# A decoder trunk's opening re-ordered: x loaded and transposed first, two conditioning blocks on TensorE, vector loads on GpSimd's queue, four gate tiles ahead

## Chip, cores and metric

One core of one Trainium2 chip. The metric is the device time of one execution in microseconds (us). A block is 128 of the 1024 model channels; there are eight.

## What is computed

One layer of a decoder trunk for 512 tokens of 1024 channels, all in float32. What matters here is its opening:

```
cond = silu(c);  sh1, sc1, gt1, sh2, sc2, gt2 = split(cond @ ada_w + ada_b)
h = rmsnorm(x, norm1_w) * (1 + sc1) + sh1
p = h @ w_in          # columns of mixers A (HGRN2), B (sparse attention), C (RWKV-7) and three gates
r, k, v, xw, xa, xg of mixer C = shift(p_c)     # p + (previous token's p - p) * mu
```

Then the three mixers run on `p`, their outputs are merged by sigmoid gates and projected, and a SwiGLU feed-forward part with a second conditioned norm follows.

## The kernel before

**Products.** A float32 product of full precision is made of three float32r products: a matrix is split into a high part (ScalarE's cast, `hi`) and the rest (VectorE's subtraction, `lo`), and hi x hi, hi x lo and lo x hi are added in PSUM (`mm3`). A weight tile of 128 output channels is therefore 8 x 3 = 24 products of 512 columns. Products of plain float32, as those with the vector `ones` or the small ones of the mixers, appear as two instructions each.

**The opening** (lines 575 to 607 of `run`, with `first_load`, `norm_x`, `first_gemm`, `modulate`). SyncE issues all loads: `c`, the conditioning weights of blocks 0 and 1 (`aw`, 1 MB a block: the columns of shift and scale, rows of 512 B), x in four row blocks, the identity, the vectors (`load_vecs`, twelve small loads in two groups), then for each further block `aw` and the 768 first columns of mixer C (`fw`, 0.4 MB), at the end constants and masks. Each row block of x is squared and summed on ScalarE, its `rs` taken to the power -0.5 on GpSimd, and scaled by VectorE and ScalarE in halves. For each of the 8 blocks VectorE forms the conditioning sums (`facc`, 8 steps of 256 columns), TensorE reduces them over the partitions by a product with `ones` (4 instructions a block), VectorE adds the bias and forms the scale `s`; TensorE transposes x's block, ScalarE applies scale and shift (`nh`) and casts (`hhi`), VectorE subtracts (`hlo`); then 18 products go into six PSUM tiles that stay open over all blocks. After the last block `c_setup` shifts the six results (ScalarE, then VectorE, for each) and applies tanh and sigmoid. In this part the framework's scheduler sets the order.

**The mixers** (line 1614 on, `manual_schedule`): the order is written out by the kernel's own planner. `Clock` keeps a planned time for each engine and buffer, from a table of costs (`count`, `spend`). `Order.run` advances *chains* (generators of narrow work: the mixers, the bias, the conditioning rows `D`, the compression `K`), each with a rank and a list of what it waits for, and *tiles* (`Weights`: load, split, 24 products) that fill TensorE in between. A chain goes first while the narrow work credited in `narrow` is below `pace`. `tend` loads up to three tiles ahead (three `wraw` buffers, two of `whi` and `wlo`) and splits the first one. A tile waits for the names in `needs`; a name is set by `mark`. The first tile is mixer A's `q` of head 0. Near the end of this part come eight tiles of the first gate (`gt`, they need `pm`, the room of the merged result) and eight compression tiles (`kt`, they need `blk`, and use their raw weights directly), in the order gt0, gt1, kt0, kt1, gt2, ..., gt5, gt6, gt7.

Of the kernel before, what the change touches and what calls it, by code (L numbers as in the profile page):

```python
# [100 lines left out]
FIRST = {k: 1 for k in range(KT)}  # L101


class Clock:
# [35 lines left out]
    def start(self, e, outs, ins):  # L140
        t = [self.ready(x) + 0.07 for x in ins] + [self.free(x) + 0.07 for x in outs]
        return max([self.at[e]] + t)

    def end(self, outs, ins, t, lag=0.0):
        for x in ins:
            for k in self.keys(x):
                self.read[k] = max(self.read.get(k, 0.0), t)
        for x in outs:
            for k in self.keys(x):
                self.wrote[k], self.by[k] = t + lag, lag > 0  # L150
        self.last = max(self.last, t + lag)

    def count(self, e, op, a, kw):
# [3 lines left out]
        t = self.start(e, outs, ins)  # L157
        n = max(int(np.prod(x.shape[1:])) for x in aps)
        if "dma" in op:
# [3 lines left out]
            self.bus = max(self.bus, t + 1.3) + size / 3.3e5  # L163
            return self.end(outs, ins, self.bus + 0.7)
# [43 lines left out]
class Order:  # L208
# [19 lines left out]
    def spend(self, o, l, r, turn=False):  # L228
# [11 lines left out]
        if kind != self.kind:  # L240
# [3 lines left out]

        t = max([clock.at["PE"]] + [clock.ready(x) + 0.07 for x in (l, r)] +
                [max(clock.read.get(x, 0.0), 0.0 if clock.by.get(x) else clock.wrote.get(x, 0.0)) + 0.07 for x in clock.keys(o)])
# [3 lines left out]
        clock.end([o], [l, r], t + c, 0.12)  # L250
# [11 lines left out]
    def mark(self, name, *aps):  # L262
        self.done[name] = max([self.at] + [self.clock.ready(x) for x in aps])
# [14 lines left out]
    def when(self, x):  # L278
        if isinstance(x, str):
            return self.clock.at["DVE"] - 0.1 if x == "dve" else self.room(x[1:]) if x[0] == ":" else self.done.get(x, 1e9)  # L280
        return self.clock.ready(x) if isinstance(x, bass.AP) else x
# [10 lines left out]
    def tend(self):  # L292

        loaded = sum(w.raw is not None and (w.w is None or w.split is None) for w in self.tiles)
        loaded += bool(self.steps and self.tile.split is None)
        for x, w in enumerate(self.tiles[:4]):
            if w.raw is None:
                if loaded >= 3:
                    break
                w.prepare(self.clock, 0)  # L300
                loaded += 1

        for x, w in enumerate(self.tiles[:3]):
            if all(n in self.done for n in w.needs):
# [3 lines left out]
        if self.tiles and all(n in self.done for n in self.tiles[0].needs):  # L308
            self.tiles[0].prepare(self.clock, 1)

    def job_ready(self):
        if self.steps:
            return 0.0
# [8 lines left out]
    def product(self):  # L322
# [4 lines left out]
        self.steps.pop(0)()  # L327
        self.narrow -= 0.8 * (self.at - t)

    def run(self, until=None, pace=4):  # L330
        while until not in self.done and (self.chains or self.tiles or self.steps):
# [23 lines left out]
class Weights:  # L355


    def __init__(self, load, split, steps, needs=(), ring="g"):
        self.load, self.split, self.todo, self.needs, self.ring = load, split, steps, needs, ring
        self.raw = self.w = self.hi = None  # L360

    def prepare(self, clock, split):
        if self.raw is None:
            self.raw = self.load()
        if split and self.w is None:
# [8 lines left out]
    def next(self, clock):  # L374

        return clock.ready(self.raw if self.hi is None else self.hi) - 0.2
# [8 lines left out]
class Trunk:  # L385
# [92 lines left out]
    def load_vecs(self, t, pool):  # L478
        nc, i = self.nc, self.i
        rows = self.t(pool, [sum(n for _, n in VTILES[t]), P], f"vrows{t}")  # L480
        for name, _ in VTILES[t]:
# [6 lines left out]
            nc.sync.dma_start(rows[r0:r0 + n], ap)  # L488
        return rows

    def turn_vecs(self, rows):
        nc = self.nc
        n = rows.shape[0]
        ps = self.psn()
        nc.tensor.transpose(ps[:, :n], rows, self.ident[:n, :n])
        vT = self.t(self.cp, [P, n], f"vT{len(self.vT)}")
        nc.vector.tensor_copy(vT, ps[:, :n])
        self.vT.append(vT)
        if len(self.vT) == 2:
# [4 lines left out]

    def setup_vecs(self):
        nc = self.nc

        self.cond = self.t(self.cp, [P, 8], "cond")
        nc.scalar.activation(self.cond, self.cT, AF.Sigmoid)
        nc.vector.tensor_tensor(self.cond, self.cond, self.cT, op=ALU.mult)  # L510
        self.adaT = self.t(self.cp, [P, 48], "adaT")
        self.mhalf = self.t(self.cp, [P, 8], "mhalf")
        nc.gpsimd.memset(self.mhalf, -0.5)
        self.ones = self.t(self.cp, [P, 1], "ones")
        nc.gpsimd.memset(self.ones, 1.0)
# [63 lines left out]
    def first_gemm(self, xs, pool):  # L579

        nc, V = self.nc, self.nc.vector
        h = self.h
        s1 = self.t(self.cp, [P, 8], "s1")
        offs = (1536, 1664, 512, 640, 0, 1024)
        pss = [self.psm(), self.psm(), self.psg(), self.psf(), self.psg(), self.psf()]
        pa, px = self.psn(), self.psn()

        def ada(k):
            if k not in self.first_a:
                return  # L590
            aw, n = self.first_a[k]
            acc = self.t(pool, [P, 2, 2, P], "facc", bufs=2)[:, :, :n]
            for kk in range(KT):
                self.ada_sum(acc, kk, aw[:, :, kk])
            for x in range(n):
                self.ada_cols(pa[:, 2 * (k + x):2 * (k + x) + 2], [acc[:, 0, x], acc[:, 1, x]], k + x, 8)
            V.scalar_tensor_tensor(s1[:, k:k + n], self.adaT[:, 8 + k:8 + k + n], 1.0, self.vec("norm1_w", k, n), op0=ALU.add, op1=ALU.mult)

        def products(ks):
            w = []  # L600
            for k in ks:
                raw = self.first_w[k]
                whi = self.t(self.wp, [P, 1024], "whi", F32R, bufs=2)
                wlo = self.t(self.wp, [P, 1024], "wlo", F32R, bufs=2)
                nc.scalar.copy(whi[:, :768], raw[:, :768])
# [1222 lines left out]
```

## Time and profile before

| | |
|---|---|
| median of 3 runs | 1171.03 us (1169.71 to 1173.94) |
| profiled execution | 1174.54 us, span 1172.6 us |
| mean granted TensorE clock | 0.983 of full speed |
| TensorE, VectorE, ScalarE, GpSimd busy | 96%, 56%, 35%, 7% of the span |

The span runs from the first to the last instruction of the profiled execution; its own time is 1.9 us longer. Times in rows are from the span's start. PE is TensorE, DVE is VectorE, ACT is ScalarE, POOL is GpSimd, SPq is the issue queue of SyncE. All engine calls but TensorE's go through a helper, so their line is L191 and products are L438; tiles are told apart by name. In a row `out<-in` names the tiles, `xN` the number of instructions merged into it, and what stands in brackets is the idle time ahead and what ended it. A product's shown duration is longer than the distance to the next one, because products are pipelined; the distance between starts is the pace.

### The profile page before, as it was taken

To read this page: it belongs to the slowest core of one execution; us is meant where nothing else is said; L and a number is where in the kernel's file an instruction comes from. 1 tells how busy PE (TensorE), PEld (TensorE's weight loads), DVE (VectorE), ACT (ScalarE), POOL (GpSimd) and SP (SyncE) were. 2 spreads that over 40 slices of the span, in tenths; PEclk is the share of its full clock that TensorE was granted. 3 is DMA by queue.
4 is the path that set the end of the run, shared out by engine and by line. 5 is a ranking of instruction groups with operands and counts; after the bars stand their busy time and mean duration, and the time that the engine had idled before them with its cause. 6 is when DMAs were issued, how large, how long until landed. Compare 5 with 4: busy or idle time off the path is not lost.

```text
span 1172.6 us, 18592 instructions
## 1 busy us (share of the span) xinstructions
PE 1120.2 (96%) x7497; PEld 912.0 (78%) x7497; DVE 656.4 (56%) x1396; ACT 412.0 (35%) x737; POOL 82.7 (7%) x96
## 2 busy tenths in 40 slices
PE   3989999999999999899999989998999999999997
PEld 3759887878887887577878758887888888888886
DVE  5858666666757766377666745446343343432533
ACT  4352421242332231155454654435232322322221
POOL 1001010120111000110112002110000000000000
PEclk9989999999999999889999999999999999999999
DMA  9934532324243244643222105542233333333231
GB/s 284 257 105 143 131 97 73 84 67 141 57 111 82 71 118 117 194 147 99 73 63 76 33 1 148 155 137 78 85 90 100 98 90 108 90 94 104 90 108 72
DMA packets 183086, 125.28 MB, mean 107 GB/s; under 512 B 27929, under 2 KB 163111, under 8 KB 183000
## 3 DMA queue, kind: packets, MB, share of 16 engines
q1 hardware_dynamic: 182424, 123.04, 37.0%
q8 instruction: 59, 0.97, 0.3%
q10 hardware_dynamic: 576, 1.05, 0.2%
q14 instruction: 27, 0.22, 0.1%
HBM read 121.15 MB, written 5.53 MB: 108 GB/s over the span
## 4 chain that ended last, share of the span: by engine, by line
PE 86%; DVE 4%; DMA 4%; SPq 2%; ACT 2%; issue 2%; POOL 0%; POOLq 0%; DVEq 0%; ACTq 0%
PE g L438 27%; PE f L438 27%; PE m L438 18%; PE n L438 11%; SPq L191 2%; PE n L442 2%; DMA adaw<-in_ada_w_dram 1%; DMA fw<-in_w_in_dram 1%; DMA wraw<-in_w_in_dram 1%; DVE wlo L191 1%; DMA x<-in_x_dram 1%; PE m L442 1%; ACT bpt L191 0%; DVE adacc L191 0%; DVE ylo L191 0%
## 5 line engine op out<-in xcount | busy, mean ns | idle before, releaser
L191 DVE TENSOR_TENSOR wlo<-wraw,whi 128x1024 fp32r<-128x1024 f32 (+2 forms) x144 | 164.1, 1139 | 158.3 <-ACT whi L191 156.5
L191 ACT CAST whi<-wraw 128x1024 fp32r<-128x1024 f32 (+2 forms) x144 | 139.1, 967 | 282.8 <-PE f L438 119.6
L438 PE MATMUL g<-hhi,whi 128*128 128x512 f32 x360 | 155.5, 432 | 9.6 <-ACT whi L191 9.6
L438 PE MATMUL g<-hhi,wlo 128*128 128x512 f32 x360 | 143.6, 399 | 1.9 <-DVE wlo L191 1.8
L438 PE MATMUL g<-hlo,whi 128*128 128x512 f32 x360 | 143.3, 398 | 0.0
L438 PEld LDWEIGHTS g<-hhi,whi 128*128 128x128 f32 x360 | 69.8, 194 | 29.5 <-ACT whi L191 10.9
L438 PE MATMUL f<-hhi,whi 128*128 128x512 f32 x232 | 91.8, 396 | 0.0
L438 PE MATMUL f<-hhi,wlo 128*128 128x512 f32 x232 | 90.9, 392 | 0.0
L438 PE MATMUL f<-hlo,whi 128*128 128x512 f32 x232 | 90.6, 390 | 0.0
L438 PEld LDWEIGHTS g<-hhi,wlo 128*128 128x128 f32 x360 | 69.0, 192 | 20.1 <-DVE wlo L191 4.7
L438 PEld LDWEIGHTS g<-hlo,whi 128*128 128x128 f32 x360 | 69.4, 193 | 11.4 <-issue 0.5
L191 DVE SCALAR_TENSOR_TENSOR adacc<-adaw,cond,adacc 128x512 f32<-128x512 f32 x56 | 42.5, 759 | 15.6 <-DMA adaw<-in_ada_w_dram 15.0
L438 PEld LDWEIGHTS f<-hhi,whi 128*128 128x128 f32 x232 | 44.3, 191 | 8.9
L438 PEld LDWEIGHTS f<-hhi,wlo 128*128 128x128 f32 x232 | 43.6, 188 | 9.0
L438 PEld LDWEIGHTS f<-hlo,whi 128*128 128x128 f32 x232 | 43.6, 188 | 8.5
L438 PE MATMUL f<-whi,hhi 128*128 128x256 f32 (+1 forms) x144 | 44.4, 308 | 0.0
L191 DVE CUSTOM_DVE_ANT_0 bs<-m,bW 128x128 f32<-128x128 f32 (+3 forms) x64 | 30.1, 486 | 24.5 <-PE m L438 15.3
L438 PE MATMUL f<-whi,hlo 128*128 128x256 f32 (+1 forms) x144 | 41.6, 289 | 0.0
L438 PE MATMUL f<-wlo,hhi 128*128 128x256 f32 (+1 forms) x144 | 41.5, 288 | 0.0
L438 PE MATMUL f<-yhi,whi 128*128 128x512 f32 x96 | 38.8, 404 | 2.2 <-ACT yhi L191 1.4
L191 ACT ACTIVATE bs<-bs,bst 128x128 f32<-128x128 f32 (+3 forms) x64 | 35.9, 563 | 12.9 <-DVE bst L191 12.4
L191 POOL TENSOR_TENSOR merged<-merged,msg 128x512 f32<-128x512 f32 x16 | 25.9, 1622 | 202.4 <-DVE msg L191 194.5
(439 smaller groups left out, 2376.8 us busy)
## 6 DMA issues: line engine op xcount, KB each, us to landing
wraw<-in_ffn_w_dram SPq DMA_DIRECT2D x66, 512.0 KB
wraw<-in_w_in_dram SPq DMA_DIRECT2D x52, 512.0 KB
adaw<-in_ada_w_dram SPq DMA_DIRECT2D x64, 256.0 KB
aw<-in_ada_w_dram SPq DMA_DIRECT2D x16, 512.0 KB
wraw<-in_w_branch_dram SPq DMA_DIRECT2D x16, 256.0 KB
wraw<-in_w_out_dram SPq DMA_DIRECT2D x8, 512.0 KB
fw<-in_w_in_dram SPq DMA_DIRECT2D x24, 128.0 KB
toep<-toep SPq DMA_DIRECT2D x8, 320.0 KB
```

Source lines behind the costliest of these rows:

```text
L191: r = f(*a, **kw)
L438: return self.nc.tensor.matmul(o, l, r, **kw)
L442: return self.nc.tensor.transpose(o, x, ident)
```

## The change

The planner now orders the opening too, as chains and tiles of the same kind. SyncE loads `c`, x and the identity first; the vectors are loaded from GpSimd's queue. Conditioning blocks 2 and 3, and 4 and 5, are formed in pairs (512 columns a step, loads of 1 KB rows); blocks 0 and 1 are not summed on VectorE but on TensorE, by 16 products of one column each. There are three buffers of two blocks' width, so the loads of block 4, 6 and 7 wait until blocks 0, 1 and 2 have been used. Row blocks 1 and 3 of x are squared on VectorE. All of x is transposed ahead into `xT`, and the modulation reads that. The products of a block stand as hi x hi, lo x hi and hi x lo in turn for all six results; in the last block they stand by result, and each result is shifted at its end (`c_first`). The first tile's split goes into buffers of its own (the later place of `bq`) as soon as the last scale exists; the bias chain waits for that tile. Four gate tiles lead, and the first may be split ahead of `pm`. `pace` is 8 instead of 4, and `mark` no longer counts TensorE's planned time. The planner's costs for transfers are changed as well.

```diff
-FIRST = {k: 1 for k in range(KT)}
+FIRST = {0: 1, 1: 1, 2: 2, 4: 2, 6: 1, 7: 1}
...
     def mark(self, name, *aps):
-        self.done[name] = max([self.at] + [self.clock.ready(x) for x in aps])
+        self.done[name] = max(self.clock.ready(x) for x in aps)
...
-    def run(self, until=None, pace=4):
+    def run(self, until=lambda: False, pace=8):
...
+            elif w.own and self.when(w.own) <= self.at:
+                w.prepare(self.clock, 1)
...
-            nc.sync.dma_start(rows[r0:r0 + n], ap)
+            nc.gpsimd.dma_start(rows[r0:r0 + n], ap)
...
-            for a in range(2):
-                nc.sync.dma_start(aw[:, a], ...)
+            for kk in ((0, 4), (4, 8)):
+                for a in range(2):
+                    nc.sync.dma_start(aw[:, a, kk[0]:kk[1]], ...)
...
+    def first_loads(self, pool, raw):
+        nc, last = self.nc, []
+        for k in range(KT):
+            if k in FIRST:
+                if len(last) > 2:
+                    yield f"a{last[-3]}"
+                last.append(k)
+                self.first_load(k, pool, True)
+            self.first_load(k, pool, False)
+        nc.sync.dma_start(self.consts, self.i["consts"][:, P:])
+        nc.sync.dma_start(raw, self.i["masks"])
+        yield raw
+        nc.gpsimd.tensor_copy(self.masks, raw)
+    def first_norm(self, xs, j, pool):
...
+        if j % 2:
+            V.tensor_tensor_reduce(self.t(pool, [P, D], "junk"), x, x, 1.0, 0.0, ALU.mult, ALU.add, ss)
+        else:
+            nc.scalar.activation(self.h[0][:, 2 * j:2 * j + 2].rearrange("p k t -> p (k t)"), x, AF.Square, accum_out=ss)
+        yield ss
+        self.rstd(rs, ss, 1.0 / D, 1e-6)
+        yield rs
...
+    def first_turn(self, xs):
...
+        yield self.ident, *(f"x{j}" for j in range(4))
...
+        for k in range(3):
+            turn(k, "mfg"[k])
+            keep(k)
+        for k in range(3, 6):
+            turn(k, "mfg"[k - 3])
+        yield "s0", ":n"
+        turn(6, "n")
+        turn(7, "n")
+        yield "hi0x"
+        for k in (5, 3, 4, 6, 7):
+            keep(k)
+        self.order.done["turned"] = self.order.at
+    def first_ada(self, pool, ks):
...
+            if k < 2:
+                ps = None
+                for q in range(2):
+                    for a in range(2):
+                        yield self.cond, aw[:, a, 4 * q:4 * q + 4], ("now", "turned")[k], ":n" if ps is None else "now"
+                        if ps is None:
+                            ps = self.psn()
+                        for kk in range(4 * q, 4 * q + 4):
+                            self.mm(ps[:, a:a + 1], aw[:, a, kk], self.cond[:, kk:kk + 1], start=(kk + a == 0), stop=(kk + a == KT))
+                self.order.done[f"a{k}"] = self.order.at
+                yield "vec0"
...
+    def first_tiles(self):
...
+                if k < KT - 1:
+                    return [(lambda q=q, x=x: (step(q, x), step(q + 1, x)), f"h{k}" if x == 2 else "now") for x in range(3) for q in (0, 2, 4)]
+                return [(lambda q=q: [step(q, x) for x in range(3)], f"h{k}") for q in range(6)]
...
+            order.chain("tx", self.first_turn(xs), 2)
+            order.chain("ada0", self.first_ada(p0, [0, 1]), 2.5, "m")
...
+            q = self.t(self.pbr, [P, 2, 1024], "bq", F32R)
+            order.job(self.a_tile("q", 0, h, (), (q[:, 0], q[:, 1])), af("f", 0), *av(0), ...
...
-            order.job(*gt[:2], *[x for n in range(4) for x in (kt[2 * n], kt[2 * n + 1], gt[2 + n])], *gt[6:])
+            order.job(*gt[:4], *[x for n in range(4) for x in (kt[2 * n], kt[2 * n + 1], gt[4 + n])])
```

## Rows read from the trace of the kernel before

**Rows 1.** The page, busy time of TensorE.

```profile
PE 1120.2 (96%) x7497; PEld 912.0 (78%) x7497; DVE 656.4 (56%) x1396; ACT 412.0 (35%) x737; POOL 82.7 (7%) x96
```

**Rows 2.** Windows: length, busy time by engine (x instructions), granted clock, DMA share, GB/s.

```profile
0.00:20.00 20.00, 2.95 (x13) 2.75 (x13) 9.81 (x29) 8.99 (x15) 2.97 (x11) 1.00 0.93 275
...
60.00:80.00 20.00, 14.62 (x54) 9.69 (x55) 10.10 (x16) 6.71 (x10) 0.12 (x1) 0.83 0.38 115
80.00:100.00 20.00, 19.37 (x136) 17.47 (x133) 15.27 (x22) 10.32 (x13) 5.73 (x7) 1.00 0.35 106
```

**Rows 3.** Timeline of TensorE in the opening: start, duration, what, idle before.

```profile
17.12 1.01 PE L438 MATMUL n<-ones,facc 128*128 128x1 f32 x4
...
21.61 1.12 PE L667 MATMUL n<-ident,x 128*128 128x128 f32 x4 [1.34 <-ACT nh L191]
...
22.38 1.20 PE L438 MATMUL m<-hhi,whi 128*128 128x512 f32 x2
...
42.76 0.50 PE L438 MATMUL n<-ones,facc 128*128 128x1 f32 x4
...
65.71 0.39 PE L438 MATMUL g<-hhi,wlo 128*128 128x512 f32 x1
...
66.16 0.39 PE L438 MATMUL f<-hhi,wlo 128*128 128x512 f32 x1
71.89 0.80 PE L438 MATMUL g<-hhi,whi 128*128 128x512 f32 x1 [5.34 <-ACT whi L191]
...
75.02 0.63 PE L438 MATMUL g<-hhi,whi 128*128 128x512 f32 x1
75.45 0.47 PE L438 MATMUL g<-hlo,whi 128*128 128x512 f32 x1
...
76.09 1.24 PE L438 MATMUL n<-bvg 33*8 33x512 f32 x4
```

**Rows 4.** Transfers to 70 us in slices of 1.75; timeline of SyncE, one issue.

```profile
GB/s 0 86 322 291 290 317 405 410 378 269 246 301 313 304 290 310 294 291 315 291 294 311 299 295 303 286 262 89 9 67 337 315 312 321 62 0 214 172 0 0
...
9.27 0.38 SPq L191 DMA_DIRECT2D vrows<-in_norm_w_dram  x1
```

**Rows 5.** Timeline and one window where gate and compression tiles meet.

```profile
475.21 1.04 ACT L191 CAST whi<-wraw 128x1024 fp32r<-128x1024 f32 x1 [5.95 <-DMA wraw<-in_w_in_dram]
476.31 0.80 PE L438 MATMUL g<-hhi,whi 128*128 128x512 f32 x1 [3.41 <-ACT whi L191]
...
476.31:482.15 5.84, 5.80 (x15) 4.22 (x16) 3.02 (x5) 0.00 (x0) 0.00 (x0) 0.53 1.04 307
...
496.64 0.37 ACT L191 ACTIVATE e<-f 62x256 f32<-62x256 f32 x1
...
506.17 0.86 PE L438 MATMUL n<-bw,e 128*128 128x64 f32 x6
```

**Rows 6.** Timeline and one window: 16 one-column instructions in a row, then the clock.

```profile
185.91 1.05 PE L438 MATMUL n<-ones,aq 128*128 128x1 f32 x8
...
186.82 1.03 PE L438 MATMUL m<-ones,adacc 128*128 128x1 f32 x8
...
188.00:190.00 2.00, 2.00 (x25) 1.39 (x25) 1.73 (x10) 0.58 (x1) 0.00 (x0) 0.57 0.08 31
```

**Rows 7.** Groups by line, to 66 us; GpSimd's `merged` and `adacc` from the page.

```profile
L191 DVE SCALAR_TENSOR_TENSOR facc<-aw,cond,facc 128x256 f32<-128x256 f32 x56 | 25.6, 482 | 0.6
...
L191 ACT ACTIVATE nh<-n,adaT,s 128x512 f32<-128x512 f32 x8 | 6.2, 777 | 19.8 <-DVE s L191 19.2 <-PE n L667 0.6
...
L191 ACT CAST hhi<-nh 128x512 fp32r<-128x512 f32 x8 | 5.0, 620 | 0.3
...
L191 POOL TENSOR_TENSOR rs<-rs,mhalf 128x1 f32<-128x1 f32 x4 | 2.6, 649 | 15.7 <-DVE rs L191 15.7
...
L191 DVE SCALAR_TENSOR_TENSOR adacc<-adaw,cond,adacc 128x512 f32<-128x512 f32 x56 | 42.5, 759 | 15.6 <-DMA adaw<-in_ada_w_dram 15.0
...
L191 POOL TENSOR_TENSOR merged<-merged,msg 128x512 f32<-128x512 f32 x16 | 25.9, 1622 | 202.4 <-DVE msg L191 194.5
```

More of the change, by code (lines that the diff above doesn't have):

```diff
@@ L292, in tend @@
     def tend(self):
-        loaded = sum(w.raw is not None and (w.w is None or w.split is None) for w in self.tiles)
+        loaded = sum(w.raw is not None and (w.w is None or w.split is None) for w in self.tiles if not w.early)
         loaded += bool(self.steps and self.tile.split is None)
@@ L307, in tend @@
                 break
-        if self.tiles and all(n in self.done for n in self.tiles[0].needs):
+        if self.tiles and (self.tiles[0].early or self.tiles[0].ahead or all(n in self.done for n in self.tiles[0].needs)):
             self.tiles[0].prepare(self.clock, 1)
@@ L312, in job_ready @@
         if self.steps:
-            return 0.0
+            x = self.steps[0]
+            return self.when(x[1]) if isinstance(x, tuple) else 0.0
         if not self.tiles:
@@ L326, in product @@
         t = self.at
-        self.steps.pop(0)()
+        x = self.steps.pop(0)
+        (x[0] if isinstance(x, tuple) else x)()
         self.narrow -= 0.8 * (self.at - t)
-    def run(self, until=None, pace=4):
-        while until not in self.done and (self.chains or self.tiles or self.steps):
+    def run(self, until=lambda: False, pace=8):
+        while not until() and (self.chains or self.tiles or self.steps):
             self.tend()
@@ L355, with __init__ @@
 class Weights:
-    def __init__(self, load, split, steps, needs=(), ring="g"):
-        self.load, self.split, self.todo, self.needs, self.ring = load, split, steps, needs, ring
+    def __init__(self, load, split, steps, needs=(), ring="g", early=False, own=None, ahead=False):
+        self.load, self.split, self.todo, self.needs, self.ring, self.early, self.own, self.ahead = load, split, steps, needs, ring, early, own, ahead
         self.raw = self.w = self.hi = None
@@ new lines, in first_mod @@
+    def first_mod(self, pool):
+        nc, h = self.nc, self.h
+        for k in range(KT):
+            yield f"s{k}", f"xT{k}"
+            f = self.t(pool, [P, T], "nh", bufs=2)
+            nc.scalar.activation(f, self.xT[k], AF.Identity, scale=self.s1[:, k:k + 1], bias=self.adaT[:, k:k + 1])
+            nc.scalar.copy(h[0][:, k], f)
+            self.order.mark(f"hi{k}", h[0][:, k])
+            self.order.done[f"hi{k}x"] = self.order.at
+            yield h[0][:, k]
+            nc.vector.tensor_tensor(h[1][:, k], f, h[0][:, k].bitcast(F32), op=ALU.subtract)
+            self.order.mark(f"h{k}", h[1][:, k])
@@ L712, in steps @@
             return [lambda k=k: step(k) for k in range(KT)]
-        return Weights(lambda: self.load_w(src, KT, P), lambda raw, hi: self.cut_w(raw, hi, KT, P), steps, needs)
+        return Weights(lambda: self.load_w(src, KT, P), lambda raw, hi: self.cut_w(raw, hi, KT, P, dst), steps, needs, ahead=early, own=f"s{KT - 1}" if dst else None)
     def proj(self, off, h, tag, n=128):
@@ L1131, in a_tile @@
         off = A_OFF + (0 if nm == "q" else 512) + 128 * hd
-        return self.full(self.i["w_in"][0, :, off:off + 128], h, end, needs)
+        return self.full(self.i["w_in"][0, :, off:off + 128], h, end, needs, dst)
     def a_mixer(self, y):
@@ L1608, in run @@
[L1608 to L1617 removed]
+            nc.scalar.activation(self.cond, self.cT, AF.Sigmoid)
@@ new lines, in run @@
+            kt, gt = self.b_compress_tiles(), self.gate_tiles(0, h)
+            order.job(*gt[:4], *[x for n in range(4) for x in (kt[2 * n], kt[2 * n + 1], gt[4 + n])])
+            order.run(lambda: f"h{KT - 1}" in order.done and not [w for w in order.tiles if w.early and w.w is None] and "vec1" in order.done)
+            ahead.close()
+            self.pc = pcs.enter_context(tc.tile_pool(name="pc", bufs=1))
+            with tc.using_default_side("right"):
+                self.pa = pas.enter_context(tc.tile_pool(name="pa", bufs=1))
```

322 lines of the change are left out of this document (173 added, 149 removed).

## The prediction, made before the change was timed

> **What bounds the kernel now.** I began with the page: TensorE is busy for 1120 of the 1172.6 us [rows 1]. So the change can give TensorE's idle gaps, and stretches in which products run at the lower clock. The windows show where these lie in the opening: 17 us of idle in the first 20, and 5.4 us between 60 and 80 at a mean granted clock of 0.83 [rows 2]. TensorE's timeline then says what they are. The first product of the opening starts at 22.38 and the last at 66.16; the next one, of the first mixer tile, has waited 5.34 us for ScalarE's `whi` and starts at 71.89 [rows 3]. Products follow each other every 0.225 us at 2.4 GHz (two steps from 65.71 to 66.16) and every 0.43 at 1.2 GHz (75.02 to 75.45) [rows 3]. The opening's 8 blocks of 18, 144 products, would take 32.4 us at the better pace and got 44.0; transposes, products of one column, waits and the clock are the rest. The transfers run at about 300 GB/s, and at 405 while x, with rows of 4 KB, is read [rows 4].
>
> After 80 us TensorE is nearly always busy (19.37 of 20 us [rows 2]), so a lead won in the opening should last unless a later gap swallows it. A later gap that the change touches stands where gate and compression tiles meet: 3.41 us of waiting before 476.31, then products at a granted clock of 0.53 [rows 5].
>
> **The start: x first.** Data begin to flow 3 us into the span [rows 4]. x is 2.1 MB, 5.2 us at 405 GB/s: it has landed near 9. Block 0 of the conditioning weights (1 MB, 3.5 us at 300 GB/s) follows, and its quarters land from about 10.2 to 12.9. From the planner's cost table in the code, used for the order alone, I read TensorE's order: three quarters of block 0's conditioning products, 24 transposes, the fourth quarter, 8 transposes, 12 products of block 0, all conditioning products of block 1, the other 6.
>
> A conditioning block is 16 products of one column, 32 instructions; four such took 1.01 us at the start and eight took 1.03 at the full clock, so 0.25 and 0.13 each [rows 3, 6]. Then: 24 at 0.25 from 10.2 end at 16.2; 24 transposes at 0.19 (four from 21.61 to 22.38 [rows 3]) at 20.8; the fourth quarter takes 1.0 to 2.0; two small VectorE steps about 0.5; `nh` and `hhi` 0.78 and 0.62 [rows 7]. The first product starts at 24.7 at the latest by this, at 23.0 if the clock rises during the transposes; I take 24.0, **1.6 us later than today**. TensorE's order sets it, not the transfers.
>
> **The blocks.** 144 products take 32.4 us. Six conditioning blocks stay on VectorE and leave 24 `ones` instructions, 0.125 each (four in 0.50 [rows 3]), 3.0 us; the second vector transpose 0.2. The transposes, today inside this stretch, are gone from it. New are block 1's 32 instructions, and here a row speaks against the change: after 16 of that kind in a row, from 185.91, the granted clock is 0.57 from 188 to 190 [rows 6]. So 20 of them count 0.13 and 12 count 0.25, 5.6 us (bounds 4.2 and 8.0), and 8 products behind them lose 0.2 each, 1.6 (0 to 3). The first 12 products follow a pause and can lose 2.4; I take 1.6. So the last product ends at 24.0 + 32.4 + 3.0 + 0.2 + 5.6 + 1.6 + 1.6 = 68.4 against 66.4 today: **+2.0 us**, between -3.6 (62.8) and +7.3 (73.7).
>
> What feeds this: VectorE's `facc` steps fall from 64 of 0.48 or less to 16 of 0.76 (as wide as `adacc`) and 16 narrow ones, 20 us instead of 30 [rows 7], and two squares of about 1.2 come in. The last conditioning data land near 47 us, the last scale follows near 50, and its products are due near 63: hidden. SyncE's queue now waits twice on TensorE, since block 4's weights take block 0's buffer and block 6's that of block 1: near 22 and 34 us, when the transfers ahead last until about 26 and 35. Behind the second wait stand blocks 6 and 7, constants, masks and the first tiles' weights, none due before 50. They cost nothing while they are that early; a wait longer by 10 us would be felt.
>
> **The vector loads on GpSimd.** Twelve small loads leave SyncE's queue (0.38 us to issue one [rows 4]) for GpSimd's, where no row shows a load. I bound one by 0.38 and by 1.62, GpSimd's costliest common instruction; I take 0.7, near the `rs` powers at 0.65, the smallest work there on loaded data [rows 7]. These four powers stand behind the loads, and all transposes wait for the last power. At 0.7 GpSimd is free at 9.3 and x normalised near 12.5; the transposes' turn is at 16.2, so nothing is lost up to 1.0 us a load.
>
> **The seam to the first tile.** Today six shifts, two functions and the tile's split follow one another on ScalarE and VectorE while TensorE waits. The change splits tile q0 into buffers of its own once the last scale exists, and shifts each product group as it ends. The gap, 66.4 to 71.89, is 5.5 us, and the low clock behind it cost 2.2: nine products from 71.89 to 76.09 took 4.2 where 2.0 would do [rows 3]. **-7.7 us**; at worst 2 us return as a wait for the second tile's split, which needs ScalarE and VectorE during the shifts. The bias products (1.24 us at 76.09 [rows 3]) move back and cost the same there.
>
> **The gates.** Four gate tiles instead of two lead, so the fourth one's weights need not wait for a buffer that compression tiles hold (its cast had waited 5.95 us for them [rows 5]). The gap of 3.41 can go, and of the 5.84 us of slow work after it (11 products, 4 transposes) about 2.7: -6.1. But one gate now follows the last compression tiles instead of three. That chain's tail lasts from the activation at 496.64 to its last products near 506.9 [rows 5]; one gate, 24 products or 5.4 us, leaves 4.9 open. I take **-1.2**, between -6.1 and +7.1 (gap kept, tail open, 2.2 of clock behind it). The other order rules (more narrow work before a tile's turn, marks without TensorE's time) add no instruction; they reshuffle the mixers, some us either way, priced at 0.
>
> **Sum.** +2.0 - 7.7 - 1.2 = -6.9 us against the profiled execution's 1174.5 (span 1172.6 and 1.9 around it), 1167.6; that execution stood 3.5 above the median of 1171.0, so **1164.1**.
>
> **The rivals.** *The clock, and slower.* The one-column products keep TensorE at 1.2 GHz, and block 1's bring it back there. If the first five blocks run so, 74 products beyond the 16 counted lose 0.2 each, and start and block 1 another 3.1: +17.9, 1182. From some 64 products at 1.2 GHz on, the whole is slower than before. For it: today's first products are slow, as are those after 71.89 and after the `ones` [rows 3, 6]. Against it: wide products brought the clock back within 3.6 us (71.89 to 75.45 [rows 3]). Chance 0.11.
>
> *GpSimd's queue.* At 1.62 a load it is free at 20.3, the powers end at 22.9, the transposes start at 23.6 instead of 16.2: +7.4, 1171.5. VectorE's work on x from 6 us on may lengthen the loads. The Trainium skill (SBUF — State Buffer, section "SBUF: two separate sides") says that loads issued by GpSimd can be held up while VectorE has the port that both share. No row here shows such a load. Chance 0.12.
>
> *The open tail,* the gap moved rather than closed: 8.3 more, 1172.4. For it: that chain is serial. Against it: other weights may be there to fill it. Chance 0.13.
>
> *The lead is given back in the mixers,* or q0's split comes late and the seam stays: 1171, from 1165 to 1177. For it, VectorE is busy for 15.27 of 20 us behind the seam; against it, TensorE is hardly idle there [rows 2]. Chance 0.16.
>
> **The numbers.** 0.48 is left for the forecast, 1158 to 1169 by itself. About 0.5%, 5.9 us, is what a measurement of this kernel can tell from no change: faster is below 1165.2, slower above 1176.9. The bounds of start, seam and gates, taken as independent about the sum, give 1156 to 1174; outside lie the clock rival and the far ends of the others. Faster, 0.50: most of the forecast, a third of the mixer case. Slower, 0.16: the clock rival and the far ends. The same, 0.34.
>
> **What would show it.** Right: one-column products ahead of the transposes, a first product near 24 and a last near 68, the next tile's product within 1 us of it, no gap at the fourth gate and a new one of some us behind the last compression tiles. Wrong: a first product after 28 (GpSimd, or the clock), products still 0.43 apart in the third block, or a lead of 5.7 us at 80 us that has shrunk at 470.

## The result, and the profile after

The changed kernel takes 1182.16 us (median of 5, 1179.88 to 1184.4) beside 1170.22 of the kernel before (median of 5): a ratio of 1.0087, with a 95% interval of 1.0065 to 1.0109 (the quotient of these two medians is 1.0102). The forecast was 1164.1, between 1156 and 1174; it had the sign wrong. The profiled execution took 1184.05 us, 9.5 more than the profiled one of before, at the same mean granted clock of 0.983.

The page has TensorE busy for 10.8 us more than before [rows 1]; over the span of 1182.3 us that leaves 51.3 us of idle time, where before had 52.4:

```profile
PE 1131.0 (96%) x7553; PEld 922.5 (78%) x7553; DVE 653.6 (55%) x1364; ACT 415.5 (35%) x740; POOL 89.4 (8%) x108
```

So, summed over the span, the time came as work on the engine that bounds the kernel. The idle time hardly shrank, because it moved. Where it went is seen when the span is cut at four points of both kernels, each the moment at which ScalarE begins to read a result: that of the first mixer tile (`q0`), of the last value tile, the first of the next stage, and the first of the feed-forward stage. Windows of the kernel before (length, busy time by engine, granted clock, DMA share, GB/s):

```profile
0.00:82.30 82.30, 56.60 (x247) 43.95 (x248) 53.27 (x122) 33.45 (x51) 4.06 (x13) 0.94 0.81 229
82.30:431.60 349.30, 345.01 (x3485) 292.12 (x3483) 233.98 (x522) 108.74 (x193) 38.62 (x43) 0.99 0.35 95
431.60:572.90 141.30, 134.70 (x1012) 101.42 (x1011) 91.25 (x242) 54.19 (x122) 10.37 (x15) 0.95 0.47 134
572.90:817.50 244.60, 236.00 (x1223) 186.82 (x1224) 141.81 (x349) 120.27 (x247) 27.45 (x21) 0.99 0.30 85
```

The same windows of the changed kernel:

```profile
0.00:84.10 84.10, 67.50 (x309) 55.38 (x310) 46.67 (x88) 41.02 (x59) 11.14 (x25) 0.94 0.69 216
84.10:442.90 358.80, 353.61 (x3706) 298.91 (x3706) 241.53 (x537) 106.70 (x192) 38.89 (x44) 0.99 0.36 96
442.90:589.60 146.70, 133.38 (x815) 99.27 (x816) 88.20 (x227) 54.06 (x122) 12.59 (x15) 0.95 0.44 129
589.60:826.90 237.30, 228.66 (x1195) 181.31 (x1196) 141.10 (x350) 118.30 (x245) 24.56 (x20) 0.99 0.30 86
```

The lengths of the middle windows can't be compared, since the order of products and mixers' steps differs (3706 instructions of TensorE stand in the second, 3485 before). The idle time, length less PE's busy time, can. Opening: 16.6 us instead of 25.7, with 10.9 more of busy time, so the first cut lies 1.8 later. Mixers: 5.2 instead of 4.3. From the last value tile to the next stage: **13.3 instead of 6.6**. Behind it 8.6 in both. Granted clocks are equal window by window. In the last three windows together TensorE is busy for 715.7 us in both, so 1.8 + 0.9 + 6.7 is 9.4, which is what the feed-forward stage starts late (826.9 against 817.5). A second profile of the changed kernel (part six) has 17.1, 4.1, 12.6 and 8.6 us of idle time: the longer end is there again, the 0.9 of the mixers is not.

The first cut needs care. TensorE itself is done with `q0` sooner than before, at 81.8 instead of 82.25 (first line: before), but ScalarE reads the result only 2.3 us later, when TensorE has long gone on:

```profile
81.86 0.39 PE L438 MATMUL g<-hhi,wlo 128*128 128x512 f32 x1
81.43 0.39 PE L448 MATMUL g<-hhi,bq 128*128 128x512 f32 x1
84.08 0.60 ACT L197 ACTIVATE aq<-g 128x512 f32<-128x512 f32 x1
```

The four bias products (1.2 us), which before stood inside `q0`, now come behind it. For the same work, then, the opening takes 0.7 us more: 9.1 less of idle time and 9.8 more of busy time.

**The opening.** TensorE's timeline (start, duration, what, idle before) answers [rows 3]:

```profile
10.57 5.25 PE L448 MATMUL n<-cond,aw 128*128 128x1 f32 x24 [0.15 <-DMA aw<-in_ada_w_dram]
...
20.40 0.95 PE L448 MATMUL n<-cond,aw 128*128 128x1 f32 x8
...
23.36 0.99 PE L448 MATMUL g<-hhi,whi 128*128 128x512 f32 x2 [1.07 <-ACT hhi L197]
...
25.62 3.63 PE L448 MATMUL n<-cond,aw 128*128 128x1 f32 x32
...
38.40 0.58 PE L448 MATMUL n<-ones,facc 128*128 128x1 f32 x4 [0.76 <-DVE facc L197]
39.23 0.61 PE L448 MATMUL n<-ones,facc 128*128 128x1 f32 x4 [0.25 <-DVE adaT L197]
41.78 1.22 PE L448 MATMUL g<-hhi,whi 128*128 128x512 f32 x2 [1.95 <-ACT hhi L197]
...
73.76 0.39 PE L448 MATMUL f<-hlo,whi 128*128 128x512 f32 x1
73.98 0.39 PE L448 MATMUL g<-hhi,bq 128*128 128x512 f32 x1
```

The first product starts at 23.36 and the next tile's follows the last one at once. Between them lies a hole: block 1's products end at 37.5, block 2's start at 41.78 and run at a granted clock of 0.50 until 47.06. The 64 conditioning instructions take 9.8 us. VectorE's and ScalarE's timelines say what block 2 waited for:

```profile
33.40 0.83 ACT L197 CAST whi<-fw 128x768 fp32r<-128x768 f32 x1 [2.25 <-DMA aw<-in_ada_w_dram]
```

```profile
26.51 0.96 DVE L197 TENSOR_TENSOR wlo<-fw,whi 128x768 fp32r<-128x768 f32 x1 [2.08 <-ACT whi L197]
...
34.26 0.96 DVE L197 TENSOR_TENSOR wlo<-fw,whi 128x768 fp32r<-128x768 f32 x1 [2.25 <-ACT whi L197]
35.14 3.11 DVE L197 SCALAR_TENSOR_TENSOR facc<-aw,cond,facc 128x512 f32<-128x512 f32 x4
...
40.06 0.16 DVE L197 SCALAR_TENSOR_TENSOR s<-adaT,vT 128x2 f32<-128x2 f32 x1
```

The last four sums of the pair 2 and 3 stand behind the cut of block 2's low half, and that cut waits for its high half, cast at 33.40. The row names a transfer, but there are two buffers for high halves, and block 0's products, which held the one that block 2 gets, end at 33.35. To 80 us VectorE stood still 13.6 us ahead of such cuts; in the same view of the kernel before (last line) this idle time is 0.0:

```profile
L197 DVE SCALAR_TENSOR_TENSOR facc<-aw,cond,facc 128x512 f32<-128x512 f32 x14 | 10.5, 749 | 0.3
L197 DVE TENSOR_TENSOR wlo<-fw,whi 128x768 fp32r<-128x768 f32 x8 | 7.7, 958 | 13.6 <-ACT whi L197 13.5
L191 DVE TENSOR_TENSOR wlo<-fw,whi 128x768 fp32r<-128x768 f32 x8 | 7.6, 953 | 0.0
```

**The end of the mixers.** What stood at [rows 5] stands 18 us later, and is longer. TensorE:

```profile
494.43 0.79 PE L448 MATMUL g<-hhi,whi 128*128 128x512 f32 x1 [4.69 <-ACT whi L197]
...
517.25 0.41 PE L452 MATMUL n<-ident,e 128*128 128x128 f32 x2 [1.88 <-DVE e L197]
...
532.69 0.48 PE L448 MATMUL m<-bkhi,bqs 128*128 128x128 f32 x1 [3.82 <-DVE bqs L197]
```

SyncE's queue and ScalarE at the first of these: the gate's load is issued at 487.01, behind loads of compression tiles, and cast at 493.34.

```profile
487.01 0.38 SPq L197 DMA_DIRECT2D wraw<-in_w_in_dram  x1
```

```profile
493.34 1.04 ACT L197 CAST whi<-wraw 128x1024 fp32r<-128x1024 f32 x1 [8.72 <-DMA wraw<-in_w_in_dram]
```

The second is the compression's tail: its transposes stand in TensorE's queue ahead of the last gate's remaining products, which wait with them. The third is for the next stage's queries, and no gate product is left to run in front of them.

### The profile page after: what moved, and what is told of

The parts are those of the page before. It is cut to its first block, busy times and chain, and to the rows that moved or that the text cites. A ratio compares the mean times of both kernels' runs of the same rounds, so it can differ in the third digit from the quotient of the medians.

```text
span 1182.3 us, 18697 instructions
## 1 busy us (share of the span) xinstructions
PE 1131.0 (96%) x7553; PEld 922.5 (78%) x7553; DVE 653.6 (55%) x1364; ACT 415.5 (35%) x740; POOL 89.4 (8%) x108
## 4 chain that ended last, share of the span: by engine, by line
PE 86%; DVE 4%; DMA 3%; ACT 2%; SPq 2%; issue 1%; POOL 1%; POOLq 0%; DVEq 0%; ACTq 0%
PE g L448 27%; PE f L448 27%; PE m L448 18%; PE n L448 11%; PE n L452 2%; SPq L197 2%; DMA aw<-in_ada_w_dram 1%; PE m L452 1%; DMA wraw<-in_w_in_dram 1%; DVE wlo L197 0%; DMA w2a<-in_nsa_pe_v_dram 0%; ACT bpt L197 0%; POOL aq L197 0%; DVE bs L197 0%; DMA bvg<-in_onehot_dram 0%
## 5 line engine op out<-in xcount | busy, mean ns | idle before, releaser
L197 DVE TENSOR_TENSOR wlo<-wraw,whi 128x1024 fp32r<-128x1024 f32 (+2 forms) x143 | 166.9, 1167 | 156.5 <-ACT whi L197 156.1
L448 PE MATMUL g<-hhi,whi 128*128 128x512 f32 x352 | 151.0, 432 | 9.6 <-ACT hhi L197 4.9
L448 PE MATMUL g<-hhi,wlo 128*128 128x512 f32 x352 | 138.5, 397 | 0.8 <-DVE wlo L197 0.7
L448 PE MATMUL g<-hlo,whi 128*128 128x512 f32 x352 | 138.4, 397 | 0.0
L448 PEld LDWEIGHTS g<-hhi,whi 128*128 128x128 f32 x352 | 67.4, 192 | 30.8 <-ACT hhi L197 6.0
L197 DVE SCALAR_TENSOR_TENSOR adacc<-adaw,cond,adacc 128x512 f32<-128x512 f32 x56 | 44.9, 802 | 22.9 <-DMA adaw<-in_ada_w_dram 22.5
L448 PEld LDWEIGHTS f<-hhi,wlo 128*128 128x128 f32 x232 | 43.8, 189 | 9.0 <-issue 0.2
L448 PE MATMUL f<-yhi,whi 128*128 128x512 f32 x96 | 39.1, 407 | 1.5 <-ACT yhi L197 1.4
```

The costliest lines, as they stand in the source:

```text
L197: r = f(*a, **kw)
L448: return self.nc.tensor.matmul(o, l, r, **kw)
```

## Experiments

Ratios are to the kernel before on the same chip, with their 95% intervals. They are not quotients of the medians and lie up to 0.24% beside them. Idle and busy times are TensorE's in the one profile of each run, between cuts at the same four results.

**One: the end of the mixers.** Four kernels, each with one edit. In the changed kernel, the gate order of before:

```diff
-order.job(*gt[:4], *[x for n in range(4) for x in (kt[2 * n], kt[2 * n + 1], gt[4 + n])])
+order.job(*gt[:2], *[x for n in range(4) for x in (kt[2 * n], kt[2 * n + 1], gt[2 + n])], *gt[6:])
```

> The changed kernel with the gate tiles in the order of before (two ahead, two at the end); all before the value tiles' end at about 420 us is unchanged. Theory (the loss is the tail: four gates ahead leave gate 5 unloaded and nothing beside the end of the compression and the next stage's preparation): the last sigmoid of the gates comes near 521 us instead of 531, the gap of 4.7 us in front of gate 5's products goes, and the time falls by 8 to 12 us, to 1170 to 1174. Rival pace (a pace of 8 lets the chains run ahead and the tiles lag, in whatever order the gates stand): 1180 to 1184, the last sigmoid still near 531. Rival opening (the loss is carried from the opening to the end): 1180 to 1184.

The kernel before with the reverse of that edit:

> The kernel before with four gate tiles ahead of the compression and none after it, nothing else. Theory: slower by 4 to 12 us (1175 to 1182), with a wait on a raw tile of weights in front of a late gate and the compression's tail uncovered. Rival pace: within 3 us of before, since at a pace of 4 the tiles are not late. Rival opening: within 3 us of before.

The pace, how much narrow work of the mixers may go ahead of a ready tile, at 4 again in the changed kernel (`pace=8` to `pace=4`), and at 8 in the kernel before:

> The changed kernel with the planner's pace at 4 again, in the opening and after it. Rival pace: 1170 to 1174, with the value tiles and the first gate 8 to 18 us earlier (first gate's sigmoid near 438 us, 455.6 now). Theory: the first gate comes earlier but gate 5 still waits for its load and the tail stays open: 1176 to 1183. Rival opening: 1180 to 1184.

> The kernel before with the planner's pace at 8 instead of 4. Rival pace: slower by 8 to 12 us, 1178 to 1182. Theory: within 4 us of before, since two gates still stand behind the compression and the next stage's preparation is covered. Rival opening: within 2 us of before.

Measured: 1184.59 us, 1.0099 (1.0071 to 1.0126), with the gate order back; 1186.07, 1.0118 (1.0086 to 1.0150), for the kernel before with four leading gates; 1183.75, 1.0092 (1.0065 to 1.0119), with the pace back; 1195.75, 1.0199 (1.0167 to 1.0230), for the kernel before at 8. Each part alone spoils the kernel before, by more than any answer had expected (at most 1182), and neither alone heals the changed one: my theory failed for the first run, the rival of the pace for the third. The rival of the opening came within a microsecond in these two and failed in the other two. The kernel before with four leading gates shows, wait for wait, the end that the changed kernel has:

```profile
492.36 0.79 PE L438 MATMUL g<-hhi,whi 128*128 128x512 f32 x1 [4.87 <-ACT whi L191]
...
516.27 0.41 PE L442 MATMUL n<-ident,e 128*128 128x128 f32 x2 [1.75 <-DVE e L191]
...
530.21 0.48 PE L438 MATMUL m<-bkhi,bqs 128*128 128x128 f32 x1 [3.80 <-DVE bqs L191]
```

Its idle time from the last value tile to the next stage is 13.4 us (6.6 before). At a pace of 8 the kernel before idles 9.0 us in the mixers and 12.2 behind them, and the mixers' clock falls to 0.95. To the feed-forward stage that is 9.7 us more of idle time and 11.6 more of busy time:

```profile
82.80:453.00 370.20, 361.20 (x3617) 306.53 (x3617) 241.34 (x536) 110.56 (x196) 39.31 (x43) 0.95 0.34 89
453.00:591.80 138.80, 126.55 (x871) 93.28 (x872) 83.20 (x227) 54.61 (x122) 10.05 (x15) 0.96 0.46 134
```

In the changed kernel with the gate order back the wait in front of a gate stays, and the idle time at the end is 13.2 us instead of 13.3:

```profile
488.64 0.80 PE L448 MATMUL g<-hhi,whi 128*128 128x512 f32 x1 [4.82 <-ACT whi L197]
```

With the pace back the gate's wait for its load is gone, but the waits of the tail and of the queries stay, at 1.95 and 3.82 us, and the idle time at the end is 12.2.

**Two: both edits undone together** in the changed kernel.

> The changed kernel with both the gate order of before and a pace of 4. Each alone gained nothing there, and each alone put into the kernel before cost 14 and 23 us. Theory now (either is enough to spoil the end of the stage, so only both together show it): 1165 to 1174, the last of the gates' sigmoids before 523 us and the next stage's first result near 573. Rival opening (the loss is carried from the opening, whatever stands at the end): 1179 to 1185 again.

Measured: 1180.81 us, 1.0041 (1.0017 to 1.0066). By the ratio half of the loss goes (by the medians two fifths: 1.0060 against 1.0102), less than expected. 13.2 us of idle time stay at the end, but of another kind: the gate's wait is gone, that for the queries is 1.21, and a chain's products wait for VectorE:

```profile
458.92 1.28 PE L448 MATMUL m<-X,GB 64*64 64x64 f32 x32 [3.66 <-DVE X L197]
```

The opening had to be looked at.

**Three: the opening,** on the kernel with both undone. First, the cut of a low half behind the sums of its own row:

```diff
-if self.tiles and (self.tiles[0].early or self.tiles[0].ahead or ...
+if self.tiles and (self.tiles[0].early in self.done or self.tiles[0].ahead or ...
...
-return [Weights(..., (f"hi{k}", "turned"), None, True) for k in range(KT)]
+return [Weights(..., (f"hi{k}", "turned"), None, f"a{k - (k in (3, 5))}" if k > 1 else "now") for k in range(KT)]
```

> As the run with both undone, but the low half of block 2's weights and of those behind it is cut on VectorE only after the sums that its own row waits for are done. Theory for the opening (VectorE's queue stood at a cut that waited for a buffer which the products of two blocks earlier held, with the pair's sums behind it): the first product of block 2, at 41.8 us in the changed kernel, comes 1.5 to 3 us earlier, the wait of 2.25 us for the high half goes from VectorE, and the last product of the opening, at 74.0, comes 1 to 4 us earlier. Rival (VectorE's sums themselves, or TensorE's lower clock, set the opening): block 2 within 1 us of 41.8, the last product within 1 us of 74.0.

Second, no pairs (`FIRST = {k: 1 for k in range(KT)}`, and six buffers of one block in place of three of two):

> As the run with both undone, but no pairs: every block's conditioning is loaded and summed by itself, blocks 0 and 1 still on TensorE. Theory for the opening (a pair's sums must all be done before the first of its two blocks can go on, and VectorE comes to them late): block 2's first product 3 to 5 us before 41.8 and the last product of the opening before 72. Rival (the pair saves VectorE 0.2 us in each of 14 steps and larger packets bring the loads earlier, so single blocks are dearer): the last product at 75 or later.

Third, block 1's conditioning back on VectorE:

```diff
-            if k < 2:
+            if k < 1:
...
-order.chain("ada0", self.first_ada(p0, [0, 1]), 2.5, "m")
-for k in list(FIRST)[2:]:
+order.chain("ada0", self.first_ada(p0, [0]), 2.5, "m")
+for k in list(FIRST)[1:]:
```

> As the run with both undone, but only block 0 has its conditioning on TensorE and block 1's sums go back to VectorE. Theory for the opening (VectorE is the engine that is late, so 3.7 us more on it delay everything behind): the last product 2 to 5 us later than in the run with both undone. Rival (the 32 narrow products between block 0's halves, 3.6 us on TensorE, and the lower clock behind them are what costs): the last product 1 us or more earlier, and a granted clock above 0.91 from 20 to 40 us.

Measured: 1179.11 us, 1.0041 (1.0017 to 1.0066); 1183.4, 1.0077 (1.0053 to 1.0100); 1182.64, 1.0061 (1.0033 to 1.0089). The totals differ too little to judge by; the openings don't. With the cut behind the sums VectorE (first fence) finishes the pair 2.7 us sooner, but the products of one column (TensorE, second fence) now stand behind block 1's:

```profile
32.42 3.10 DVE L197 SCALAR_TENSOR_TENSOR facc<-aw,cond,facc 128x512 f32<-128x512 f32 x4
35.44 0.95 DVE L197 TENSOR_TENSOR wlo<-fw,whi 128x768 fp32r<-128x768 f32 x1
```

```profile
37.49 0.62 PE L448 MATMUL f<-hlo,whi 128*128 128x512 f32 x2
37.95 0.50 PE L448 MATMUL n<-ones,facc 128*128 128x1 f32 x4
...
41.26 1.22 PE L448 MATMUL g<-hhi,whi 128*128 128x512 f32 x2 [1.95 <-ACT hhi L197]
```

Block 2 comes only 0.5 us sooner (the rival's answer), the last product 2.6 (the theory's, 71.4 against 74.0): the clock came back at 44 instead of 47, the later waits shrank. What is left of the hole is no longer VectorE's queue: 3.3 us lie between the first products of one column (37.95) and block 2's first product (41.26), a chain of two such sums, bias, scale, modulation and cast. Without pairs the last product ends at 75.9, so the pairs are not shown to be the fault. With block 1 back on VectorE it ends at 72.7, 1.5 before the 74.2 of the kernel it was put in, where I had expected 2 to 5 later: for block 1's work TensorE, to which the change moves it, was the dearer place. The clock was not the reason: from 20 to 40 us it was 0.87, and 0.91 in the changed kernel. Single profiles scatter: in the eight with the opening as changed the last product ends between 73.9 and 75.7. So 71.4 and 72.7 are clear of that, and 75.9 hardly is.

**Four: another pace.** The gate order of before with a pace of 5; with the two mends of the opening besides; four leading gates at a pace of 5; and the mended opening, gate order of before, at 7.

> The changed kernel with the gate order of before and a pace of 5, which lays the mixers' products out in an order nearer to that of before (about 80 per cent of TensorE's instructions stand in the same order, 70 with a pace of 4 or 8). Theory (the end of the mixers, where the chains and the tiles must run out together, decides, and the opening with its seam is worth about nothing): level with before, a ratio of 0.997 to 1.003, chain C's last result near 466 us and the last gate near 521. Rival (the loss is carried from the opening): a ratio of 1.004 to 1.010, as with the other paces.

> As the last, with the opening mended in two places: only block 0's conditioning on TensorE, and the low halves of blocks 2 and on cut behind the sums that they wait for. Theory: the opening's last product comes 2 to 4 us before that of the last run, q0's tile ends before 81 us, and the time is 2 to 4 us less, below before: ratio 0.993 to 1.000. Rival (what the opening gains, the mixers give back, as with the seam): the same time as the last run within 1.5 us.

> The changed kernel with a pace of 5 alone: four gate tiles lead, none stands behind the compression. Against the run with the gate order of before and the same pace it tells the price of the gate order alone. Theory: 4 to 12 us slower than that run (the kernel before lost 14 with this order), the next stage's first tile end (573 us before) 8 to 15 us later, with a wait of over 3 us on a gate's load. Rival (the pace is the whole cause): within 2 us of that run.

> The mended opening and the gate order of before, but a pace of 7 in place of 5. Theory (the pace decides how far the tiles run ahead of chain C, and any pace that ends the two apart loses): chain C's last result after 475 us, a stretch of TensorE under 16 of 20 us between 440 and 480, and 4 to 10 us slower than with a pace of 5. Rival (pace matters little once the opening is mended): within 2 us of that run.

Measured: 1186.56 us, 1.0085 (1.0050 to 1.0120); 1176.04, 1.0023 (1.0001 to 1.0046); 1182.54, 1.0074 (1.0051 to 1.0096); **1166.91, 0.9954 (0.9930 to 0.9978)**. An order like that of before did not bring the time of before, and at 5 the gate order of before gained nothing (1186.56 against 1182.54 with four leading gates; the rival had named a difference within 2 us). The mended opening was worth 0.6%, TensorE ending `q0` at 77.4 instead of 83.6. The last run I had expected to lose, and it is the fastest: chain C ends late, at 473 us, near the 475 that I had named, but the tiles are so early (last value tile at 411.8) that TensorE finds work: it is busy for 18.4 and 18.8 of the 20 us on either side of 460, not under 16. Its windows:

```profile
0.00:80.60 80.60, 64.26 (x281) 52.08 (x282) 50.70 (x96) 41.00 (x58) 11.19 (x25) 0.94 0.71 226
80.60:411.80 331.20, 328.47 (x3254) 279.54 (x3253) 224.11 (x508) 100.58 (x182) 38.67 (x41) 1.00 0.37 97
411.80:568.90 157.10, 147.78 (x1252) 112.12 (x1251) 102.66 (x258) 59.20 (x132) 14.62 (x17) 0.98 0.45 133
568.90:809.70 240.80, 231.79 (x1209) 184.15 (x1210) 141.42 (x348) 118.29 (x245) 26.97 (x21) 0.99 0.30 86
```

16.3, 2.7, 9.3 and 9.0 us of idle time, 37.4 to the feed-forward stage against 45.2 before and 43.8 in the changed kernel, and its busy time of 772.30 is that of before again. Against the mended opening at a pace of 5 the gain is not idle time, which was 38.1 us there, but busy time, which was 781.0, at granted clocks of 0.98 and 0.96 in the two middle windows where the fastest kernel has 1.00 and 0.98.

**Five: the shares.** From the fastest kernel one part is taken back each time: the opening (as changed, unmended); pace and gate order (the mended opening alone in the changed kernel); the gate order. The fourth is the kernel before at a pace of 7.

> The changed kernel with its own opening, the gate order of before and a pace of 7: the fastest run so far without the mended opening. Theory (the opening as changed costs 3 to 5 us against the mended one, and the rest is the order at the end): 3 to 6 us slower than the fastest run, a ratio of 0.998 to 1.002 to before. Rival (the end alone decides): 0.993 to 0.997, as that run.

> The changed kernel with the mended opening alone; pace 8 and four leading gate tiles stay. Theory: q0's tile ends 3 to 4 us before the changed kernel's 84.1, and the time is 3 to 6 us below it, a ratio of 1.003 to 1.006; TensorE's idle time from the last value tile to the next stage's first result stays near 13 us. Rival (the opening is the whole loss): 0.996 to 1.000. Rival (what the opening gains is given back): 1.007 to 1.010.

> The fastest run (mended opening, pace 7) with the four leading gate tiles of the change again. Theory (four in front leave nothing beside the end of the compression): 3 to 10 us slower than the fastest run, a wait of over 3 us on a late gate's high half and one of over 3 us on the queries of the next stage. Rival (with the tiles early enough the gate order is free): within 2 us of it, 0.993 to 0.997.

> The kernel before with a pace of 7 instead of 4, nothing else. Theory (its order was the fitting one at 4, as the 23 us lost at 8 showed): slower by 5 to 20 us, a ratio of 1.004 to 1.017. Rival (7 is the better pace whatever the opening): 0.990 to 0.997.

Measured: 1174.42 us, 1.0017 (0.9994 to 1.0041); 1177.65, 1.0048 (1.0027 to 1.0070); 1175.68, 1.0021 (0.9997 to 1.0045); 1189.0, 1.0146 (1.0111 to 1.0180). All four ratios lie where the theory said. The pace alone doesn't do it, and each part has its price: the opening 0.63% of the time (1.0017 less 0.9954), four leading gates 0.67%, and pace 8 instead of 7 another 0.27% (1.0048 less 1.0021; these intervals overlap). TensorE's time to the feed-forward stage, in us, from one profile each:

| kernel | idle | of it at the end of the mixers | busy |
|---|---|---|---|
| before | 45.2 | 6.6 | 772.3 |
| changed | 43.8 | 13.3 | 783.1 |
| fastest | 37.4 | 9.3 | 772.3 |
| fastest with the opening as changed | 37.9 | 9.1 | 774.8 |
| fastest with four leading gates | 42.2 | 14.1 | 775.5 |
| mended opening alone | 42.2 | 13.4 | 778.6 |
| before, pace 7 | 51.0 | 6.7 | 780.9 |

In these profiles the gates' price is idle time at the end (4.7 us more). The opening's is mostly work, but that profile, at 1169.8 us, lies 4.6 under the median of its kernel and shows only a part of it.

TensorE with four leading gates, and the fastest run, at the same places:

```profile
482.74 0.80 PE L448 MATMUL g<-hhi,whi 128*128 128x512 f32 x1 [3.27 <-ACT whi L197]
...
522.10 0.47 PE L448 MATMUL m<-bkhi,bqs 128*128 128x128 f32 x1 [3.80 <-DVE bqs L197]
```

```profile
488.49 0.50 PE L448 MATMUL g<-hhi,wlo 128*128 128x512 f32 x1 [0.85 <-DVE wlo L197]
514.82 0.45 PE L448 MATMUL m<-bkhi,bqs 128*128 128x128 f32 x1 [3.34 <-DVE bqs L197]
```

Here the wait for a gate's load comes with the four leading gates; in the changed kernel's own opening it stood with either order at a pace of 8 and with neither at 4. The wait for the queries stays in both, so that one is not theirs here, though at 8 and at 4 it was (3.82 with four leading gates, 1.21 with two).

**Six: once more,** the fastest kernel and the changed one on one chip.

> The fastest kernel once more (mended opening, gate order of before, pace 7), in more rounds. Theory: a ratio of 0.993 to 0.998 to before, with its interval below 1. Rival (it was the pick of many): 0.998 to 1.003.

> The changed kernel once more, on the same chip as the last. Theory: 1.007 to 1.011 to before. Rival (its loss hung on the one chip): 1.000 to 1.005.

Measured: 1167.76 us, 0.9954 (0.9940 to 0.9968), and 1181.26, 1.0076 (1.0052 to 1.0099). The fastest version beats both kernels, and with the same ratio as at first, so it was not just the pick of many. Of the 7.6 us between the changed kernel and the one before, some 2 go with the granted clock (0.9855 in the mean of its executions against 0.9874), an estimate at a microsecond for each 0.001 (last section).

## Why the prediction was wrong, step by step

- **The start: right.** Forecast 24.0, measured 23.36. The conditioning products took a little less than counted (24 in 5.25 us where 6.0 stood, 8 in 0.95 where 1.0 to 2.0 did).
- **The blocks: the step that failed is "What feeds this" and its "hidden".** Last product forecast at 68.4, measured 74.0, beyond my worst bound of 73.7. I compared the sums' total on VectorE with the time to hand, but neither the order in its queue nor the chain from a block's sums to its first product, which stands in TensorE's queue behind the block ahead (3.3 us even with VectorE's order mended). From first product to last took 50.6 us where the sum has 44.4. TensorE idled 5.05 of it (50.62 less 45.57 busy), where 0 was priced, and the 12 products behind the longest wait lost 2.6 (5.28 us at 0.50). Block 1's 32 instructions, priced at 5.6, took 3.63 and give 2.0 back. That is 5.65 of the 6.2 more; the rest are small terms either way. The runs of the third and fifth part show that the opening's order costs time, and that moving block 1's conditioning to TensorE was no gain.
- **The seam: right.** The next tile's product starts 0.22 us behind the last, at the full clock: nearly all of the -7.7. With the blocks 7.6 later than before it only paid for them: for the same work the opening is 0.7 longer where I had -5.7.
- **The gates: "the fourth one's weights need not wait" failed, and "-1.2" with it.** The wait of 3.41 [rows 5] in front of the fourth gate moved to the sixth, again the second behind compression tiles, and grew to 4.69, and the tail stood open: 6.7 us more idle time at the end. That was my worst bound (+7.1). Its price is shown in two kernels: the one before with this order alone has the same three waits and 1.2%, and the fastest loses 0.67% by it. In the changed kernel itself the 6.7 can't be put down to the gates alone: with their order back 13.2 us stay idle, because a pace of 8 is enough for that (12.2 in the kernel before), and at a pace of 5 four leading gates cost nothing.
- **"They reshuffle the mixers, some us either way, priced at 0" failed.** The pace alone cost the kernel before 1.46% at 7 and 1.99% at 8, more than half of it as busy time at a lower clock. In the changed kernel its part is not seen by itself: a pace of 4 alone gained nothing, the 0.9 us more idle time in the mixers did not come again, and 7 and 8 differ by 0.27% with the opening mended.
- **The sum.** 6.4 for the opening, 7.9 for the end of the mixers, 0.9 for their idle time and 1.0 of busy time behind `q0`, for which I have no cause, on top of -6.9 make +9.3; measured +9.4 at the feed-forward stage.
- **The range** took start, seam and gates as independent. One planner lays out all of them, and two bad ends came together.
- **The rivals.** *The clock* named 1182, the time that came, by another way, so that was luck: the granted clock to 84 us is 0.94 in both kernels. Behind block 1's products it did fall, to 0.60 from 29.38 to 33.16, and ten products lost 1.5 us, as the sum had it (1.6). The break-even named there was summed wrongly: 64 slow products lead to 1176.9, and some 35 to the time of before. *GpSimd's queue* did not decide: its loads cost 0.52 us each (the first 0.75), against the 0.7 taken, and the powers start at 9.66:

```profile
5.79 0.52 POOL L197 DMA_DIRECT2D vrows<-in_rw_r_k_dram  x1
7.25 0.52 POOL L197 DMA_DIRECT2D vrows<-in_rw_lnx_w_dram  x1 [0.94 <-DMA vrows<-in_ada_b_dram]
...
9.66 3.40 POOL L197 TENSOR_TENSOR rs<-rs,mhalf 128x1 f32<-128x1 f32 x4
```

  Nothing in these rows shows the hold that the Trainium skill (SBUF — State Buffer, "SBUF: two separate sides") tells of; the two longer gaps end with earlier loads. From issue to landing the loads took 4.1 to 5.7 us, those of x on SyncE's queue 4.9 in the median, and whether a hold hides in the former is not shown. *The open tail* came true in its mechanism, and together with the lost opening. *The lead given back* did not come to be tested: there was no lead.

**What stays open:** why a pace of 5 with the gate order of before is slow (1.0085). It is not idle time, of which it has 39.1 us to the feed-forward stage against 45.2 before, but busy time, 792.5 against 772.3, at a clock with a mean of 0.977 over its executions against 0.987. What lowered it was not tried, nor was a fourth raw buffer for the gates' loads. The other parts of the change (`mark`, the planner's costs for transfers, the loads on GpSimd's queue, the squares on VectorE) stand in the fastest kernel too and were not tried alone.

## What to carry to other kernels

When an engine is 96% busy, set the idle time that a change removes against the work that it puts on that engine: here the opening's idle time fell by 9.1 us, and its busy time rose by 9.8 for the same work. For each in-order queue write down what stands behind an instruction that can wait, above all a cut "ahead of time" whose buffer is still in use. Where one planner orders a whole stage, a knob of it is a change of its own, and its bounds are not independent of the rest: measure the parts one by one and in pairs, since either of two faults can hide the cure of the other.

## What the runs showed of the hardware

Thirty-two products of one column in a row took 3.63 us right behind wide products (0.113 each), and 24 of them ahead of the transposes 5.25 (0.22 each); the granted clock of both stretches is 1.00, so the rows don't tell why. Behind the 32 it was 0.60 for the next 3.8 us. Executions of one and the same program differ in the granted clock and in time with it: of the kernel before, on one chip, between 1168.2 us at a mean of 0.992 and 1180.2 at 0.981, about a microsecond for each 0.001. So a difference under half a per cent takes many executions here, and one profile may stand some us from the median.
